# Two up products of an encoder layer: weight sums on another engine, raw weights in other memory, first-half norms in groups, and a sum of squares in two parts

## The chip, the cores and the metric

The kernel runs on one core of one Trainium2 chip. A core has TensorE (PE, matmuls), VectorE (DVE), ScalarE (ACT), GpSimd (POOL) and SyncE (SP, which issues DMAs); each takes its own instructions in program order and waits on semaphores for the others. The metric is the device time of one execution in microseconds (us).

## The reference

One layer of a bidirectional encoder in float32, for 1024 positions and 16 meta tokens in front (1040 rows), width 1024:

```
h += 0.5 * SwiGLU_1(RMSNorm(h))
u  = RMSNorm(h);  z = u @ W_in       # two head groups, differential and windowed attention
h += concat(A, RMSNorm(B)) @ W_out
h += 0.5 * SwiGLU_2(RMSNorm(h))      # then a final RMSNorm
swiglu(x) = (silu(x @ w_gate) * (x @ w_up)) @ w_down      # 1024 -> 2816 -> 1024
rmsnorm(x) = x * rsqrt(mean(x * x) + 1e-6) * g
```

The change is in the two products with `w_gate` and `w_up`, here called the up products.

## The kernel before

**Numbers in halves.** A float32 product is made of three products of high and low parts: `split` makes `hi` by a ScalarE copy and `lo = src - hi` on VectorE (L117 and L114 in the profile; `tt`, L114, is every two-operand sum or difference). An operand is ready for the third pass only with its low part, the remainder.

**The up product.** `ffn_up` is called twice, with 520 rows in a half (two matmuls of 260 columns a step) and with 512. It takes gate and up together as a block product by fewer multiplications: for each of 22 tiles `f` of 128 output columns the weights are four blocks, `a11`, `a12` (the raw tile `rg` of `w_gate`) and `a21`, `a22` (the raw `ru` of `w_up`), and seven products of sums of blocks stand for eight. The sums of weights are `s1 = a21 + a22`, `s2 = s1 - a11`, `a21 = a11 - a21` (written over `ru`, so it appears as `ru<-rg,ru`) and `s4 = a12 - s2` (`s<-rg,s`). Their high and low halves are the tiles `wah`/`wal` (raw `a11`, `a12`, and the first tile's `s2`, `s1`), `wbh`/`wbl` (`s2`, `s1` of later tiles) and `wch`/`wcl` (`a21`, `s4`, `a22`). For the first tile, `f = 0`, `s1` and `s2` are made early by `first_sums` on VectorE; all else is made by GpSimd in the tile loop. The products are in L226, what they leave in PSUM is taken by VectorE into `u` and `g` and by ScalarE into `m` and `sg`.

**The sums of activations.** The other operands are blocks of the normed input: `b11` and `b21` of the first half of the rows, `b22` and `t1` to `t4` of both halves. `prepare` (`prepare1`, `prepare2`) makes the first half, its norm and the splits into `b11` and `b21`; `combine` makes the second half and the rest in `second_half`. The input tiles are called `ha`, `hc` (first half) and `hb`, `hd` (second half), `x2` is a temporary. A norm is a sum of squares over 1024 (squares on ScalarE, the sum over partitions by a matmul with ones), then `newton` (L139 to L142: two steps on ScalarE, the first with a table load, and two on VectorE, written `nr` and `ns`), then one VectorE operation for each tile, `normed` (L149). In the first product `rstd_each` squares eight tiles and lets TensorE add them all, in the second the squares are added on VectorE.

**Order.** `lead_a` and `lead_b` do for the first five tiles the two products that need only `b11` and `b21` and raw blocks, so that TensorE has work while `combine` makes the rest (`early_work` deals them out). A scheduler puts the instructions of each engine in order before the program runs, and small edits change its order. Memory is taken in rings, reserved by name in the order of a table; the rings `la4` of the tile loop lie where the preparation's tiles (`nsq`, `nacc`, `ns`, `nr`, `x2`, `ha` to `hd`) lay, so a load or a split into `la4` waits until the last reader of the tile that was there is done.

Of the kernel before, what the change touches and what calls it, by code (L numbers as in the profile page):

```python
# [10 lines left out]
F32 = mybir.dt.float32  # L11
F32R = mybir.dt.float32r
AF = mybir.ActivationFunctionType
ALU = mybir.AluOpType
# [4 lines left out]
P = 128  # L19
D = 1024  # L20
KT = D // P
# [30 lines left out]
def layer(  # L52
# [4 lines left out]
    nc = tc.nc  # L57
# [55 lines left out]
    def tt(eng, out, a, b, op):  # L113
        eng.tensor_tensor(out, a, b, op=op)  # L114
# [75 lines left out]
    def ffn_up(H, wg, wu, nlead, prepare, combine, accs):  # L190
# [5 lines left out]
        with ExitStack() as st:  # L196
# [103 lines left out]
            for tag, bufs in (  # L300
                ("rg0", 1), ("ru0", 1), ("wbh", 2), ("wbl", 2), ("rg1", 1), ("ru1", 1),
                ("u2", 1), ("m5", 1), ("u3", 1), ("wch", 3), ("wcl", 3), ("g", G_BUFS),
            ):
                la4.reserve(tag, bufs)
# [9 lines left out]
            for f in range(FT):  # L314
# [28 lines left out]
                product(p3, weight(la4, "wb", s1, 2) if f else first["ws1"], "t1", True)  # L343
                tt(gp, a21, a11, a21, ALU.subtract)
                m5 = tmp(la5, "m5")
# [4 lines left out]
                if nxt is not None:  # L350
                    lead_b(nxt, src)
                tt(gp, s4, a12, s2, ALU.subtract)
                product(p3, weight(la5, "wc", s4, 3), "b22", False)
# [37 lines left out]
    def first_half(hts, gi, r, blk):  # L391
        hk = KT // 2
        for k in range(KT):
            hi, lo = blk["b11" if k < hk else "b21"]
            normed(hts[k], hts[k], gi, k, r)
            split(hi[:, k % hk, :], lo[:, k % hk, :], hts[k])
            yield

# [267 lines left out]

    def rstd_each(srcs, n, width, pool, subs, full):

        for i, s in enumerate(srcs):
            sq = pool.tile([P, 520], F32, tag="nsq", name="nsq")[:, :n]  # L670
            nc.scalar.activation(sq, s, AF.Square)
            for o, (c0, cn) in subs:
                nc.tensor.matmul(o, ones, sq[:, c0 : c0 + cn], start=i == 0, stop=i == len(srcs) - 1)
        return newton(n, width, pool, full)

    def prepare1(pool, psum, blk, ps_tile, subs):
# [9 lines left out]
        outs, full = ps_tile("p2")  # L686
        r = rstd_each(a, H, D, pool, list(zip(outs, subs)), full)
        for _ in first_half(a, 0, r, blk):
# [572 lines left out]
    def prepare2(pool, psum, blk, ps_tile, subs):  # L1261
# [3 lines left out]
        with ExitStack() as st_w:  # L1265
            wp = Rings(st_w, "wo2")
            blocks = iter(())
            for half in range(2):
                sl = slice(half * H, (half + 1) * H)
                hs = []  # L1270
                for m in range(KT):
# [15 lines left out]
                    hs.append(t)  # L1287
                    next(blocks, None)
                halves.append(hs)
                if half == 0:  # L1290
# [130 lines left out]
```

## Time and profile before

| what | before |
|---|---|
| time, median of 3 runs | 2092.57 us (2092.17 to 2096.58) |
| the profiled execution's own time | 2091.47 us |
| its span in the profile | 2089.7 us (1.8 us lie around it) |
| mean granted clock of TensorE | 0.973 |
| busy: TensorE / VectorE / ScalarE / GpSimd | 1956.9 / 1262.0 / 882.8 / 993.3 us |

TensorE is busy for 94% of the span. The two up products begin at 24.38 and 1381.44 us of the span. A row of the timeline says when an operation began, how long it took, its engine, line and tiles, and in brackets how long the engine had been idle before it and what ended that. The clock is given as a share of full speed.

### The profile page before, as it was taken

The numbers are of one execution on the slowest core, as the hardware profiler recorded it, in microseconds if no ns is written. First come the engines' busy times: TensorE is split into PE (matmuls) and PEld (weight loads), VectorE is DVE, ScalarE is ACT, GpSimd is POOL, SyncE is SP. The second block draws the span as 40 slices with busy tenths as digits, with TensorE's granted clock in tenths as the row PEclk, the third lists the DMA queues.
The fourth block names the chain that finished last, engine by engine and source line by source line (L and its number), as shares of the span: only waits on it lengthen the run. The fifth ranks groups of instructions, "written<-read, shape, count | busy, mean of one in ns | idle before, by whom it ended". The sixth has DMA issues, their size and how long they took to land. (4 is left out here: it accounts for less than half of the span.)

```text
span 2089.7 us, 30414 instructions
## 1 busy us (share of the span) xinstructions
PE 1956.9 (94%) x11508; PEld 1701.2 (81%) x11508; DVE 1262.0 (60%) x1843; ACT 882.8 (42%) x1611; POOL 993.3 (48%) x811
## 2 busy tenths in 40 slices
PE   6999999998999989899978898897999999989998
PEld 5999999998999879778756677675788888867877
DVE  6755555548874661276668677466655455487745
ACT  6433333334432431366566666353333333344433
POOL 0555554545443740576446442017754554454543
PEclk8999999999999999999979999998999999999999
DMA  4332322328422351544443321522333233385122
GB/s 157 110 118 97 117 91 99 108 94 314 153 62 81 130 165 62 152 118 121 109 102 91 83 75 53 194 92 81 122 106 111 86 106 112 116 297 166 61 81 81
DMA packets 106002, 244.14 MB, mean 117 GB/s; under 512 B 14208, under 2 KB 29008, under 8 KB 105856
## 3 DMA queue, kind: packets, MB, share of 16 engines
q1 hardware_dynamic: 94336, 204.53, 30.9%
q0 software_dynamic: 11520, 37.67, 4.6%
q8 instruction: 90, 1.47, 0.3%
q14 instruction: 56, 0.46, 0.1%
HBM read 169.86 MB, written 65.44 MB: 113 GB/s over the span
## 5 line engine op out<-in xcount | busy, mean ns | idle before, releaser
L226 PE MATMUL p<-t_hi,wch 128*128 128x260 f32 (+1 forms) x528 | 142.9, 325 | 9.4 <-DVE u L114 9.4
L226 PE MATMUL p<-b_hi,wah 128*128 128x260 f32 (+1 forms) x528 | 144.4, 328 | 7.0 <-ACT b_hi L117 3.8
L226 PE MATMUL p<-b_hi,wal 128*128 128x260 f32 (+1 forms) x528 | 142.3, 325 | 6.4 <-DVE wal L114 6.4
L226 PE MATMUL p<-b_lo,wah 128*128 128x260 f32 (+1 forms) x528 | 143.7, 325 | 0.0
L226 PE MATMUL p<-t_lo,wch 128*128 128x260 f32 (+1 forms) x528 | 142.2, 324 | 0.0
L226 PE MATMUL p<-t_hi,wcl 128*128 128x260 f32 (+1 forms) x528 | 141.9, 323 | 0.0
L114 DVE TENSOR_TENSOR u<-p,m 128x520 f32<-128x520 f32 (+1 forms) x88 | 61.0, 693 | 129.2 <-PE p L226 129.1
L114 POOL TENSOR_TENSOR ru<-rg,ru 128x512 f32<-128x512 f32 x44 | 87.6, 1990 | 106.8 <-DVE hb L149 74.0
L226 PE MATMUL p<-t_hi,wbh 128*128 128x260 f32 (+1 forms) x504 | 133.7, 321 | 2.6 <-ACT wbh L117 2.6
L226 PE MATMUL p<-t_lo,wbh 128*128 128x260 f32 (+1 forms) x504 | 135.9, 320 | 0.0
L226 PE MATMUL p<-t_hi,wbl 128*128 128x260 f32 (+1 forms) x504 | 133.3, 320 | 0.0
L117 ACT CAST wch<-ru 128x512 fp32r<-128x512 f32 x88 | 54.8, 623 | 183.8 <-issue 89.5
L574 PE MATMUL pA<-bh,wh 128*128 128x260 f32 (+1 forms) x432 | 116.3, 323 | 5.4 <-DVE h L581 5.4
L117 ACT CAST wbh<-s 128x512 fp32r<-128x512 f32 x84 | 52.3, 622 | 152.1 <-PE p L226 137.3
L574 PE MATMUL pA<-bl,wh 128*128 128x260 f32 (+1 forms) x432 | 115.5, 321 | 0.0
L114 POOL TENSOR_TENSOR s<-ru 128x512 f32<-128x512 f32 x42 | 57.4, 1368 | 120.3 <-DMA ru<-wu 60.9
L574 PE MATMUL pA<-bh,wl 128*128 128x260 f32 (+1 forms) x432 | 112.3, 319 | 0.0
L114 DVE TENSOR_TENSOR bl<-r,bh 128x520 fp32r<-128x520 f32 (+1 forms) x126 | 109.9, 907 | 2.3 <-ACT bh L117 2.0
L114 POOL TENSOR_TENSOR s<-wr 128x384 f32<-128x384 f32 x48 | 55.2, 1153 | 114.0 <-DVE wl L114 94.2
L117 ACT CAST wh<-s 128x384 fp32r<-128x384 f32 x96 | 49.1, 515 | 136.8 <-PE pA L574 66.6
L581 DVE SCALAR_TENSOR_TENSOR h<-pA,h 128x520 f32<-128x520 f32 (+1 forms) x96 | 66.2, 691 | 63.1 <-PE pA L574 63.0
L117 ACT CAST wah<-rg 128x512 fp32r<-128x512 f32 x88 | 54.4, 621 | 117.9 <-PE p L226 89.2
(289 smaller groups left out, 6128.0 us busy)
## 6 DMA issues: line engine op xcount, KB each, us to landing
rg<-wg SPq DMA_DIRECT2D x44, 512.0 KB, 3.6
ru<-wu SPq DMA_DIRECT2D x44, 512.0 KB, 5.2
wr<-wd SPq DMA_DIRECT2D x24, 768.0 KB, 4.4
r<-g_t SPq DMA_DIRECT2D x12, 780.0 KB, 5.9
r<-g_t SPq DMA_DIRECT2D x12, 768.0 KB, 5.8
g_b<-g POOLq DMA_DIRECT2D x27, 260.0 KB, 5.2
r<-g_b SPq DMA_DIRECT2D x9, 780.0 KB, 4.9
g_b<-g POOLq DMA_DIRECT2D x27, 256.0 KB, 5.5
```

The lines of the kernel that those rows point to most:

```text
L114: eng.tensor_tensor(out, a, b, op=op)
L117: nc.scalar.copy(hi, src)
L226: nc.tensor.matmul(o, w_k(ww, k), x[:, k, c0 : c0 + cn], start=first and k == 0 and i == 0, stop=k == hk - 1 and i == 2, skip_group_check= ...
L574: nc.tensor.matmul(o, w_k(ww, k), xx[:, c0 : c0 + cn], start=new and k == 0 and q == 0, stop=k == DNG - 1 and q == 2, skip_group_check=not ...
L581: nc.vector.scalar_tensor_tensor(hs, full, 0.5, hs, op0=ALU.mult, op1=ALU.add)
```

## The change

Four edits, all at the starts of the up products.

1. The rings `rg1` and `ru1` (raw weights of odd tiles) are reserved ahead of `wbh` and `wbl`, so they lie on other tiles of the preparation.
2. For `f = 0` the two sums `a21 = a11 - a21` and `s4 = a12 - s2` are made by VectorE; for later tiles by GpSimd as before.
3. `first_half` norms a group of four tiles and then splits it, for `b11` and then for `b21`, in twice as many steps; `prepare2` takes two steps where it took one.
4. `prepare1` adds its squares by `rstd_pair` (two accumulators, adds on VectorE, then the matmuls with ones), which the second half already used; `rstd_each` is gone.

```diff
             for tag, bufs in (
-                ("rg0", 1), ("ru0", 1), ("wbh", 2), ("wbl", 2), ("rg1", 1), ("ru1", 1),
+                ("rg0", 1), ("ru0", 1), ("rg1", 1), ("ru1", 1), ("wbh", 2), ("wbl", 2),
                 ("u2", 1), ("m5", 1), ("u3", 1), ("wch", 3), ("wcl", 3), ("g", G_BUFS),
...
-                tt(gp, a21, a11, a21, ALU.subtract)
+                tt(gp if f else nc.vector, a21, a11, a21, ALU.subtract)
...
-                tt(gp, s4, a12, s2, ALU.subtract)
+                tt(gp if f else nc.vector, s4, a12, s2, ALU.subtract)
...
     def first_half(hts, gi, r, blk):
         hk = KT // 2
-        for k in range(KT):
-            hi, lo = blk["b11" if k < hk else "b21"]
-            normed(hts[k], hts[k], gi, k, r)
-            split(hi[:, k % hk, :], lo[:, k % hk, :], hts[k])
-            yield
+        for n, ks in (("b11", range(hk)), ("b21", range(hk, KT))):
+            hi, lo = blk[n]
+            for k in ks:
+                normed(hts[k], hts[k], gi, k, r)
+                yield
+            for k in ks:
+                split(hi[:, k % hk, :], lo[:, k % hk, :], hts[k])
+                yield
...
-        r = rstd_each(a, H, D, pool, list(zip(outs, subs)), full)
+        r = rstd_pair(a, H, D, pool, list(zip(outs, subs)), full)
...
                     next(blocks, None)
+                    next(blocks, None)
```

The order of the instructions changes with it. On VectorE at the start of the second product, behind the last two norms (`hb`, `hd`) of the second half, there stood before:

```order
L149 SCALAR_TENSOR_TENSOR hd_15521<-hd_15521,gains_64,nr_15752 128x512
L114 TENSOR_TENSOR ha_15124<-hb_15381,ha_15124 128x512
L114 TENSOR_TENSOR ha_15147<-hb_15401,ha_15147 128x512
L114 TENSOR_TENSOR b22_lo_15576<-hd_15461,b22_hi_15572 128x512
L114 TENSOR_TENSOR ha_15170<-hb_15421,ha_15170 128x512
```

and now:

```order
L149 SCALAR_TENSOR_TENSOR hd_15514<-hd_15514,gains_64,nr_15746 128x512
L114 TENSOR_TENSOR ha_15118<-hb_15375,ha_15118 128x512
L114 TENSOR_TENSOR ru_16063<-rg_16061,ru_16063 128x512
L114 TENSOR_TENSOR ha_15141<-hb_15394,ha_15141 128x512
L114 TENSOR_TENSOR b22_lo_15570<-hd_15455,b22_hi_15566 128x512
```

The sum `ru<-rg,ru` of the first tile, which GpSimd had, is the second row behind the norms; the other moved sum, `s<-rg,s`, is row 34 behind these norms, and the two remainders `wcl` that TensorE needs from them are rows 43 and 44.

On ScalarE, behind the last sigmoid before the second half's norm, there stood before:

```order
L252 ACTIVATE sg_15775<-p1_15705 128x512
L117 CAST wah_15837<-rg0_15835 128x512
L139 ACT_TABLE_LOAD
L139 ACTIVATE nr_15752<-p2_15726,eps_66 128x512
L140 ACTIVATE ns_15751<-nr_15752 128x512
```

and now:

```order
L252 ACTIVATE sg_15769<-p1_15699 128x512
L139 ACT_TABLE_LOAD
L139 ACTIVATE nr_15746<-p2_15720,eps_66 128x512
L117 CAST wah_15831<-rg0_15829 128x512
L140 ACTIVATE ns_15745<-nr_15746 128x512
```

The copy `wah` of a raw weight stood ahead of the table load and the step L139; it now stands between L139 and L140.

On VectorE in the first product, from the third row that makes `t1_lo` on, there stood before, up to the fourth of the weight remainders made from raw blocks in this stretch:

```order
L114 TENSOR_TENSOR t1_lo_322<-ha_208,t1_hi_318 128x520
L114 TENSOR_TENSOR hb_226<-hd_234,hb_226 128x520
L114 TENSOR_TENSOR hc_212<-hc_212,x2_601 128x520
L114 TENSOR_TENSOR t1_lo_322<-ha_210,t1_hi_318 128x520
L114 TENSOR_TENSOR t2_lo_330<-x2_601,t2_hi_326 128x520
L114 TENSOR_TENSOR wal_650<-rg0_647,wah_649 128x512
```

and now:

```order
L114 TENSOR_TENSOR hb_224<-hd_232,hb_224 128x520
L114 TENSOR_TENSOR t1_lo_316<-ha_208,t1_hi_312 128x520
L114 TENSOR_TENSOR hb_226<-hd_234,hb_226 128x520
L114 TENSOR_TENSOR t1_lo_316<-ha_210,t1_hi_312 128x520
L114 TENSOR_TENSOR wal_644<-rg0_641,wah_643 128x512
L114 TENSOR_TENSOR hc_212<-hc_212,x2_595 128x520
L114 TENSOR_TENSOR wal_684<-rg0_681,wah_683 128x512
```

The last row before and the last but two now are the remainder of the same block of weights. From the first norm of the second half (`hb`) to it, that row included, there were 32 rows and are 29: one remainder (`wal_536`, now `wal_530`) went ahead of the norms, and `hc` and `t2_lo` of the first tile went behind it. The first tile's sum `ru<-rg,ru` stands ahead of these norms, among the remainders `b_lo` of the first half.

On SyncE the load of the second tile's `ru` waits for another VectorE row than before: in the second product for the fourth `t2_lo` and no longer for the fourth `x2` and a copy, in the first product likewise for the fourth `t2_lo` instead of the fourth `x2`.

## Rows read from the trace of the kernel before

**Rows 1.** Busy time by stretches: stretch, its us, each engine's busy us, clock, DMA share.
```profile
0.00:50.00 50.00, 30.92 (x158) 26.49 (x159) 33.85 (x55) 30.61 (x51) 4.35 (x10) 0.85 0.46 162
50.00:100.00 50.00, 45.97 (x356) 45.12 (x355) 39.99 (x55) 22.27 (x39) 26.61 (x18) 0.95 0.30 101
100.00:150.00 50.00, 50.00 (x420) 50.00 (x419) 28.44 (x41) 16.79 (x29) 28.63 (x28) 1.00 0.37 128
1345.00:1395.00 50.00, 49.50 (x213) 39.56 (x212) 33.63 (x53) 21.63 (x36) 0.00 (x0) 1.00 0.35 127
1400.00:1450.00 50.00, 33.59 (x111) 23.58 (x111) 39.41 (x61) 23.31 (x40) 36.29 (x9) 0.83 0.20 68
```

**Rows 2.** TensorE's timeline, second product: start, us, line, tiles, [idle before <-releaser].
```profile
1432.13 0.79 PE L226 MATMUL p<-b_hi,wch 128*128 128x512 f32 x1 [5.47 <-ACT wch L117]
...
1436.27 0.80 PE L226 MATMUL p<-t_hi,wch 128*128 128x512 f32 x1 [0.79 <-DVE u L114]
...
1440.13 0.79 PE L226 MATMUL p<-t_hi,wbh 128*128 128x512 f32 x1 [2.64 <-ACT wbh L117]
...
1444.56 0.44 PE L226 MATMUL p<-t_lo,wch 128*128 128x512 f32 x1
...
1455.97 0.50 PE L226 MATMUL p<-t_hi,wbh 128*128 128x512 f32 x1
```

**Rows 3.** GpSimd's timeline, second product.
```profile
1404.94 25.25 POOL L114 TENSOR_TENSOR ru<-rg,ru 128x512 f32<-128x512 f32 x1 [74.00 <-DVE hb L149]
1430.15 1.27 POOL L114 TENSOR_TENSOR s<-rg,s 128x512 f32<-128x512 f32 x1
1438.16 1.26 POOL L114 TENSOR_TENSOR s<-ru 128x512 f32<-128x512 f32 x1 [6.74 <-issue]
```

**Rows 4.** VectorE's timeline, second product.
```profile
1401.40 0.75 DVE L149 SCALAR_TENSOR_TENSOR hb<-hb,gains,nr 128x512 f32<-128x512 f32 x1
...
1406.70 1.29 DVE L114 TENSOR_TENSOR ha<-hb,ha 128x512 f32<-128x512 f32 x2
...
1428.38 0.69 DVE L114 TENSOR_TENSOR hc<-hc,x 128x512 f32<-128x512 f32 x1
1432.63 0.69 DVE L114 TENSOR_TENSOR t_lo<-x,t_hi 128x512 fp32r<-128x512 f32 x1 [3.56 <-ACT t_hi L117]
```

**Rows 5.** ScalarE's timeline, second product.
```profile
1393.62 1.09 ACT L252 ACTIVATE sg<-p 128x512 f32<-128x512 f32 x2
1396.14 0.62 ACT L117 CAST wah<-rg 128x512 fp32r<-128x512 f32 x1 [1.43 <-DMA rg<-wg]
1396.78 1.28 ACT L139 ACT_TABLE_LOAD   x1
...
1430.22 0.62 ACT L117 CAST wch<-ru 128x512 fp32r<-128x512 f32 x1 [4.11 <-POOL ru L114]
```

**Rows 6.** TensorE's timeline, first product.
```profile
47.15 0.51 PE L226 MATMUL p<-b_hi,wal 128*128 128x260 f32 x2 [1.77 <-DVE wal L114]
...
57.51 0.51 PE L226 MATMUL p<-b_hi,wal 128*128 128x260 f32 x2 [2.67 <-DVE wal L114]
...
77.87 0.50 PE L226 MATMUL p<-t_hi,wch 128*128 128x260 f32 x2 [1.32 <-DVE u L114]
```

**Rows 7.** VectorE's timeline, first product.
```profile
36.44 1.71 DVE L149 SCALAR_TENSOR_TENSOR hb<-hb,gains,nr 128x520 f32<-128x520 f32 x1
...
56.78 0.68 DVE L114 TENSOR_TENSOR wal<-rg,wah 128x512 fp32r<-128x512 f32 x1
...
73.11 3.48 DVE L114 TENSOR_TENSOR wcl<-ru,wch 128x512 fp32r<-128x512 f32 x2
```

**Rows 8.** GpSimd's timeline, first product.
```profile
36.30 1.29 POOL L114 TENSOR_TENSOR ru<-rg,ru 128x512 f32<-128x512 f32 x1 [32.17 <-DMA ru<-wu]
```

**Rows 9.** SyncE's queue: issue of loads, both products.
```profile
63.58 0.33 SPq L311 DMA_DIRECT2D ru<-wu  x1
...
1432.35 6.02 SPq L311 DMA_DIRECT2D ru<-wu  x2
```

More of the change, by code (lines that the diff above doesn't have):

```diff
@@ L665, in rstd_pair @@
         return newton(n, width, pool, full)
[L667 to L674, printed above, removed]
     def prepare1(pool, psum, blk, ps_tile, subs):
```

## The prediction

> **What bounds the kernel now.** I read four views in this order. The table by stretches of 50 us first: TensorE is full (50.00 of 50) with the clock at 1.00 in 100 to 150 us, and short of work in two places, the first 100 us and 1400 to 1450 us, where it is busy for 30.92, 45.97 and 33.59 us and the clock falls to 0.85, 0.95 and 0.83 [rows 1]. Both are the starts of an up product: there the inputs are normed and split on VectorE and ScalarE while TensorE already wants them. An edit to these starts pays what TensorE waits less there, so that is read from its waits.
>
> The second view is the timeline of those waits. In the second up product TensorE waits 5.47 us for the high half of a weight sum, 0.79 us for a VectorE sum and 2.64 us for the next tile's high half [rows 2]; in the first, 1.77 and 2.67 us for a weight remainder (`wal`) and 1.32 us for `u` [rows 6].
>
> The third is what stands behind the longest of them. GpSimd's one subtraction `ru<-rg,ru` runs from 1404.94 for 25.25 us, and the like sum after it takes 1.27 us [rows 3]. VectorE, in the same time, runs 36 operations back to back from 1406.70 to 1428.38, 0.602 us apart [rows 4]: it is not slowed, GpSimd is kept out, and the subtraction ends 1.1 us after VectorE's run does. ScalarE's copy then starts at 1430.22, after 4.11 us [rows 5], VectorE's next remainder at 1432.63 [rows 4], TensorE at 1432.13 [rows 2].
>
> The Trainium skill, "SBUF — State Buffer", section "SBUF: two separate sides", says that VectorE and GpSimd share one pair of ports as an exclusive lock, held for a whole instruction, also where a VectorE instruction has two SBUF inputs. The trace agrees in both directions: 25.25 us on GpSimd's side [rows 3], and on VectorE's a first norm of 1.71 us beside a GpSimd sum [rows 7, 8].
>
> The fourth is the order of the two programs (the pieces above), in which I count rows and give each the duration that the trace has for its kind.
>
> **The second up product.** (a) *Its start.* In the new order ScalarE's table load and reciprocal-root step (L139) stand ahead of the copy `wah`, which waited 1.43 us for its load and held them. The table load can start at 1394.71, where the last sigmoid ends, instead of 1396.78; the copy (about 0.5 us) now falls between L139 and L140 [rows 5]. That is 2.07 - 0.5, and I take 1.45 us for VectorE's norms, from 1401.40 to 1399.95; the bound is 0, if TensorE's sum isn't ready or a load is late.
>
> (b) *The two sums on VectorE.* Eight norms take 1406.70 - 1401.40 = 5.30 us [rows 4], so they end at 1405.25. From there to the last remainder that TensorE needs (`wcl` of the second sum) the new order has 44 rows, both moved sums among them, and no GpSimd row that they wait for: 44 x 0.602 = 26.5, so 1431.75. Each sum thus costs VectorE 0.60 us on the path and takes the GpSimd wait away. With that remainder TensorE has done as many matmuls as it had at 1436.27 [rows 2]: a gain of 4.5 us. New, shorter waits will lie ahead of it (about 2 us each, for the high half at 1427.7 and for this remainder); they are inside the 4.5.
>
> (c) *Raw weights of tile 1.* The load of its `ru` was issued at 1432.35 [rows 9] and GpSimd's sum of it started at 1438.16 [rows 3]: 5.8 us. In the new order it waits for the fourth `t2_lo` of VectorE, row 40 of the 44: 1405.25 + 24.1 = 1429.4. With the same 5.8 us it lands at 1435.2; the sum (1.27) and the copy (0.5) give the high half at 1437.0. TensorE wants it 22 matmuls after 1431.75, at 0.233 us each 1436.9, later at half clock. The 2.64 us go.
>
> (d) *The clock.* In the profile, 58 matmuls lie between 1436.27 and tile 2's row at 1455.97. At 0.233 us (the pitch at full clock) they are 13.5 us; they took 19.7. Of the 6.2 lost, 2.64 are the wait, 0.75 two matmuls at half clock before it, 2.1 the ten from 1440.13 to 1444.56 (4.43 us), 0.7 spread after [rows 2]. TensorE still has waits before 1431.75, so I keep the 2.1 and the 0.7 and drop the 0.75. Sum: 4.5 + 2.64 + 0.75 = **7.9 us**. Bounds: no half clock at all, 10.7; no gain at the start, twice the half-clock loss and 0.5 us left of the wait, 7.9 - 1.45 - 2.1 - 0.5 = 3.9.
>
> **The first up product.** *The sum by two accumulators* puts adds on VectorE and takes 24 of 32 ones-matmuls off TensorE. It starts no sooner: the inputs land too late, and ScalarE's L139 step now stands behind a square of the second half. I get the first norm 0.7 us later; but of three VectorE rows between norms and remainders (0.6 each) one is left, so the remainders start 0.5 us earlier. TensorE's gain from that ends in its next wait for `wal`, hence 0 by itself.
>
> *VectorE's run.* Ahead of the second half's norms now stand the `ru` sum and one `wal` (+1.2), less the 0.5: they start at 37.1 instead of 36.44 (+0.7). The GpSimd sum at 36.30, beside which the first norm took 1.71 us [rows 7, 8] and not 0.75 as others do [rows 4], is gone (-1.0). To the `wal` for which TensorE waited 2.67 us there are 29 rows instead of 32, by the order: -3 x 0.6 = -1.8. It starts 2.1 us earlier, at 54.7 [rows 7], and TensorE goes on at 55.4 instead of 57.51 [rows 6].
>
> *The wait for `u`* (1.32 us): `u` was behind two remainders of 3.48 us, slowed beside GpSimd's sums [rows 7]. In the new order it is 28 rows behind that `wal`, ahead of all that need GpSimd's tile-1 sums: 54.7 + 28 x 0.6 = 71.5, ready at 72.2. TensorE asked 19.0 us after that `wal` (77.87 - 1.32 - 57.51 [rows 6]), half-clock loss included, so now at 74.4. The wait goes. The load of tile 1's `ru` becomes later here, behind VectorE's fourth `t2_lo` (66.9 instead of 63.58 [rows 9]): this load isn't helped by the new order of memory. Its sum would be ready near 73, and TensorE needs it near 83. Sum: 2.1 + 1.3 = **3.4 us**; bounds 0 (the `wal`s that follow become late in their turn) and 5.5 (2.1 of half clock gone too).
>
> **Norms before splits, twice as many steps in the second preparation:** TensorE is busy 49.50 of 50 us there [rows 1], so I take 0, within 0.3 either way; the work that hides it is the output projection's matmuls.
>
> **Sum.** 7.9 + 3.4 = 11.3 us off the profiled execution's 2091.47 is 2080.2; that execution lay 1.1 below the median of 2092.57, so **2081.3**. Behind both places TensorE is full, so I see nothing that gives it back. What a measurement here can tell from no change is 0.2%, 4.2 us.
>
> **Rivals.**
> 1. *VectorE becomes the bound.* It takes two sums more, is continuous from 1399.95 to 1433, and what it makes late is the next remainder. For: TensorE's wait on VectorE's `u` [rows 2] and on `wal` [rows 6], and the lower bounds of both places. Against: GpSimd's 25 us cost more than two rows. Time: 2092.57 - 3.9 = 2088.7.
> 2. *The stall moves to GpSimd's next sum,* tile 1's `s<-ru`, kept out by VectorE's run. For: 25.25 us [rows 3], and a run two rows longer. Against: its load lands when the run ends. If it costs 2 us at each place: 2085.3. By the rule of the lock it would end at most one sum after the run.
> 3. *The other side: TensorE's clock stays at half* behind the new waits. At half a matmul of 512 columns takes 0.44 us against 0.233 [rows 2]. The 11.3 us are gone when 54 more of them run at half than now. If all 58 of the second place do (48 more, 10 us) and 140 of the first (0.1 us each at half the columns, 14, of which 2 are lost now): 2092.57 - 11.3 + 22 = 2103. Against: the longest such stretch is 4.4 us in rows 2, behind longer waits.
> 4. *It does not last:* TensorE comes to a later point earlier and waits there for a load or a sum that is tied to something else. Time about 2091. Against: it is full from 100 us on [rows 1].
>
> **How the numbers follow.** Forecast 0.70, rival 1 0.13, rival 2 0.06, rival 3 0.04, rival 4 0.07. Faster by over 0.2% (below 2088.4): forecast, rival 2 and half of rival 1, 0.83; within 0.2%: the rest of rival 1 and rival 4, 0.13; slower: 0.04. The range takes the upper bounds of both places together, 10.7 + 5.5, to 2076.4, and rival 1 at the other end, 2088.7.
>
> **What would show it.** Right: no GpSimd subtraction over 5 us in the second start; the norms there 1.45 us earlier (beside the 3.4 of the first place); TensorE's 5.47 us replaced by two waits of about 2; the 2.64 gone; tile 2 some 8 us earlier against the product's start. In the first product that `wal` near 55 and no wait for `u`. Wrong: waits on `wal` or `t_lo` that grow by as much, a GpSimd sum of over 5 us elsewhere, or a half-clock stretch over 5 us behind the new waits.

## The result and the profile after

The changed kernel takes 2072.26 us (median of 4 runs, 2068.98 to 2074.79) against 2092.37 of the kernel before in the same comparison (4 runs, 2090.39 to 2096.58): a ratio of 0.9904, 95% interval 0.9886 to 0.9922. It is faster, by 20.1 us where 11.3 were forecast, and lies 4.1 us below the forecast range. The two profiled executions took 2091.47 and 2074.79 us, 16.7 apart. The other 3.4 us are where they stand in their runs: the one of before is 0.9 under its median, the one of after 2.5 over its own.

Where the 16.7 lie is read by matching matmuls, counted back from the end of each product, in the two timelines. TensorE is 3.4 us earlier after the start of the first product, 5.8 at the first matmul of the down product behind it, 7.2 when the second product's preparation takes its last sum, 16.3 behind the start of that product (from 1521 us of the profile before on), and 16.7 at the end.

The stretches of 50 us of the changed kernel, to be read beside [rows 1] (columns: stretch, its us, busy time of TensorE, its weight loads, VectorE, ScalarE, GpSimd, clock, DMA share):

```profile
0.00:50.00 50.00, 26.72 (x140) 22.33 (x140) 38.22 (x64) 30.59 (x52) 3.05 (x9) 1.00 0.52 178
50.00:100.00 50.00, 46.41 (x378) 45.47 (x378) 40.53 (x56) 22.48 (x40) 25.50 (x19) 1.00 0.28 96
1390.00:1440.00 50.00, 40.16 (x148) 29.12 (x147) 43.64 (x67) 26.36 (x44) 14.30 (x10) 0.90 0.23 74
```

From 50 to 100 us TensorE does 378 matmuls where it did 356, and the clock is 1.00 in both early stretches. In the second product's start (the window is taken 10 us earlier, as the norms come 9.9 us earlier) it does 148 where it did 111, and GpSimd's busy time falls from 36.29 to 14.30 us with one instruction more.

TensorE's timeline in that start, the answer to [rows 2]:

```profile
1399.23 0.50 PE L226 MATMUL p<-b_hi,wah 128*128 128x512 f32 x1 [1.47 <-ACT sg L252]
...
1419.25 0.50 PE L226 MATMUL p<-b_hi,wch 128*128 128x512 f32 x1 [1.90 <-ACT wch L117]
...
1423.54 0.80 PE L226 MATMUL p<-b_hi,wcl 128*128 128x512 f32 x1 [1.31 <-DVE wcl L114]
...
1427.12 0.40 PE L226 MATMUL p<-b_lo,wch 128*128 128x512 f32 x1
```

The 5.47 us for `wch` have become 1.90 and, for the remainder behind it, 1.31; the 2.64 us for `wbh` are gone; the half clock behind the waits ends at 1427.12, 3.6 us after the second. GpSimd, VectorE and ScalarE in the same place ([rows 3], [rows 4], [rows 5]):

```profile
1425.62 1.30 POOL L114 TENSOR_TENSOR s<-ru 128x512 f32<-128x512 f32 x1 [101.04 <-DMA ru<-wu]
```

```profile
1391.48 0.75 DVE L149 SCALAR_TENSOR_TENSOR hb<-hb,gains,nr 128x512 f32<-128x512 f32 x1
...
1397.39 0.68 DVE L114 TENSOR_TENSOR ru<-rg,ru 128x512 f32<-128x512 f32 x1
...
1416.66 0.68 DVE L114 TENSOR_TENSOR s<-rg,s 128x512 f32<-128x512 f32 x1
...
1422.80 0.68 DVE L114 TENSOR_TENSOR wcl<-s,wch 128x512 fp32r<-128x512 f32 x1
```

```profile
1386.42 1.28 ACT L139 ACT_TABLE_LOAD   x1
...
1388.30 0.61 ACT L117 CAST wah<-rg 128x512 fp32r<-128x512 f32 x1
```

GpSimd has no sum until 1425.62, and that one takes 1.30 us. Each moved sum takes VectorE 0.68 us. From the first norm to the end of the remainder VectorE takes 32.0 us; the forecast had 31.8 (1399.95 to 1431.75). The first norm is 9.9 us earlier than in [rows 4]: 7.2 by the earlier arrival and 2.7 here. The copy `wah` stands behind L139's step, as the order said.

The first product, on TensorE and on VectorE ([rows 6], [rows 7]):

```profile
45.70 0.51 PE L226 MATMUL p<-b_hi,wal 128*128 128x260 f32 x2 [1.98 <-DVE wal L114]
...
55.46 0.51 PE L226 MATMUL p<-b_hi,wal 128*128 128x260 f32 x2 [1.94 <-DVE wal L114]
```

```profile
37.16 0.75 DVE L149 SCALAR_TENSOR_TENSOR hb<-hb,gains,nr 128x520 f32<-128x520 f32 x1
...
54.73 0.68 DVE L114 TENSOR_TENSOR wal<-rg,wah 128x512 fp32r<-128x512 f32 x1
...
72.36 0.70 DVE L114 TENSOR_TENSOR u<-p,m 128x520 f32<-128x520 f32 x1 [0.55 <-PE p L226]
```

The norms start at 37.16 (forecast 37.1), the `wal` at 54.73 (54.7), TensorE goes on at 55.46 (55.4), and `u` is ready before TensorE asks.

The end of the first product was in no group of rows. TensorE's wait there, before and after:

```profile
487.34 0.51 PE L226 MATMUL p<-t_hi,wch 128*128 128x260 f32 x2 [3.73 <-DVE u L114]
```

```profile
482.62 0.50 PE L226 MATMUL p<-t_hi,wch 128*128 128x260 f32 x2 [2.41 <-DVE u L114]
```

The last product of a tile, `t4`, adds onto the accumulator that VectorE must first have read into `u`. That read stands, in VectorE's order, behind splits of the down product.

### The profile page after: what moved, and what is told of

It reads as the page before. It is cut to its first block, busy times and chain, and to the rows that moved or that the text cites. A ratio compares the mean times of both kernels' runs of the same rounds, so it can differ in the third digit from the quotient of the medians.

```text
span 2072.9 us, 30356 instructions
## 1 busy us (share of the span) xinstructions
PE 1943.9 (94%) x11484; PEld 1692.1 (82%) x11484; DVE 1279.3 (62%) x1853; ACT 879.4 (42%) x1611; POOL 960.3 (46%) x807
## 3 DMA queue, kind: packets, MB, share of 16 engines
q8 instruction: 90, 1.47, 0.3%
## 4 chain that ended last, share of the span: by engine, by line
PE 70%; DVE 11%; DMA 6%; ACT 5%; POOL 3%; issue 3%; SPq 1%; DVEq 0%; POOLq 0%; ACTq 0%
PE p L226 35%; PE pA L577 7%; PE pj L167 5%; PE pC L577 3%; PE pv L884 3%; PE pd L167 2%; PE ds L780 2%; DVE bl L114 2%; PE po L167 2%; PE do L1183 2%; PE pB L577 2%; PE do L167 1%; DMA ru<-wu 1%; POOL s L114 1%; ACT dp L786 1%
## 5 line engine op out<-in xcount | busy, mean ns | idle before, releaser
L114 DVE TENSOR_TENSOR wal<-rg,wah 128x512 fp32r<-128x512 f32 x88 | 74.0, 847 | 63.6 <-ACT wah L117 63.6
L117 ACT CAST wch<-ru 128x512 fp32r<-128x512 f32 x88 | 54.7, 621 | 130.5 <-PE p L226 72.6
L114 POOL TENSOR_TENSOR s<-wr 128x384 f32<-128x384 f32 x48 | 55.4, 1157 | 100.6 <-DVE wl L114 89.7
```

The lines of the kernel that those rows point to most:

```text
L117: nc.scalar.copy(hi, src)
```

## The experiments

In the tables each time is a median, beside that of the kernel before on the same chip. Places are differences of matched matmuls against the profile of before, in us (minus is earlier). "First start" is read behind the start of the first product, where the difference no longer changes (150 to 450 us of the profile before), "first end" at the first matmul of the down product; "second start" is counted from the second preparation's last sum to the stretch from 1521 to 1639 us of the profile before, where the differences hold still again.

| run | time | before | ratio (95%) | first start | first end | second start |
|---|---|---|---|---|---|---|
| e1 before again | 2092.05 | 2090.82 | 1.0012 (1.0002 to 1.0021) | -0.1 | +0.2 | -0.3 |
| e2 sums alone | 2083.46 | 2090.82 | 0.9968 (0.9957 to 0.9980) | +0.2 | +0.3 | -6.0 |
| e3 all but sums | 2078.66 | 2090.82 | 0.9939 (0.9918 to 0.9961) | -2.2 | -4.6 | -6.4 |
| e4 one sum alone | 2091.26 | 2090.82 | 1.0001 (0.9989 to 1.0013) | -0.5 | -0.2 | -0.7 |
| e5 rings alone | 2081.58 | 2091.69 | 0.9943 (0.9924 to 0.9962) | -1.7 | -2.5 | -4.0 |
| e6 norms alone | 2087.77 | 2091.69 | 0.9982 (0.9969 to 0.9996) | -0.4 | +0.7 | -2.4 |
| e7 pair alone | 2088.42 | 2091.69 | 0.9986 (0.9974 to 0.9999) | -1.7 | -0.5 | -0.5 |
| e8 all but norms | 2076.96 | 2091.69 | 0.9924 (0.9906 to 0.9941) | -3.5 | -5.8 | -5.2 |
| e9 all but rings | 2081.29 | 2091.62 | 0.9948 (0.9934 to 0.9962) | -1.4 | -1.3 | -9.6 |
| e10 all but pair | 2078.23 | 2091.62 | 0.9938 (0.9921 to 0.9955) | +1.3 | +0.2 | -8.1 |
| e11 low parts on GpSimd | 2076.18 | 2091.62 | 0.9930 (0.9915 to 0.9945) | -1.7 | -2.7 | -7.0 |
| e12 changed again | 2071.95 | 2091.62 | 0.9912 (0.9897 to 0.9927) | -2.2 | -4.6 | -9.0 |
| e13 rings, second product only | 2085.19 | 2090.26 | 0.9977 (0.9966 to 0.9987) | -0.5 | +0.7 | -3.7 |
| e14 before, own accumulator | 2091.82 | 2090.26 | 1.0006 (0.9993 to 1.0019) | -0.2 | -1.5 | -1.3 |
| e15 changed, own accumulator | 2075.41 | 2090.26 | 0.9929 (0.9915 to 0.9942) | -2.7 | -3.8 | -8.9 |

The first profile of the changed kernel, the one of the section on the result, has -3.4, -5.8 and -9.1 in the last three columns.

**e1 and e12: what two profiles of one kernel differ by.** No edit.

> The kernel of before, unchanged, profiled once more. Of the profiled gain of 16.7 us, 2.5 lie at the end of the first up product, where TensorE waits 3.73 us for VectorE's last sum in before and 2.41 us in the changed kernel, and about 1 us in the down product behind it. Theory (these belong to the change): the wait at the end is again 3.7 us within 0.3, and the median within 0.2% of before. Rival (such waits vary from run to run): the wait at the end differs by over 1 us from 3.73, and stages between 490 and 1390 us shift by 1 us or more against the first profile.

> The changed kernel once more, for the spread of its profile. Theory: its stages are within 1 us of the first profile up to 500 us and inside the second product; what differs lies in the attention stage between 730 and 1320 us, by 1 to 3 us as in the two profiles of before. Rival: the stages at the products' starts differ by over 1 us too, and then the single terms can't be read to better than that.

In e1 the wait at the first product's end is again 3.73 us, as its theory says. In e12 the first start differs by 1.2 us from the first profile, so there the rival holds, and the clock of the first 100 us is another one:

```profile
0.00:50.00 50.00, 27.09 (x137) 22.60 (x137) 37.60 (x63) 30.05 (x51) 3.06 (x9) 0.83 0.53 178
50.00:100.00 50.00, 47.03 (x371) 46.20 (x372) 39.72 (x56) 22.74 (x40) 25.22 (x18) 0.97 0.30 95
```

So the 1.00 and 1.00 of the first profile are not the change's. The places move by up to 1.3 us between two profiles of the same kernel, the stretches behind them (attention, the second down product) by up to 3, and single runs of one kernel by up to 14 (e9: 2073.82 to 2088.22). So a place is read to about 1 us, and what an edit is worth in all is read from medians. These have an error too: the unchanged kernel of e1 lies 1.2 us off itself, with an interval that does not take in 1. The gain came again: 2071.95.

**e2, e3, e4: the sums.**

```diff
-                tt(gp, a21, a11, a21, ALU.subtract)
+                tt(gp if f else nc.vector, a21, a11, a21, ALU.subtract)
-                tt(gp, s4, a12, s2, ALU.subtract)
+                tt(gp if f else nc.vector, s4, a12, s2, ALU.subtract)
```

e2 is the kernel before with both pairs of lines, e4 with the first pair alone, e3 the changed kernel without both.

> Only the first tile's two weight sums go to VectorE; rings, norms and the sum of squares stay as before. Theory (GpSimd is kept out by VectorE's run, and that is most of the gain in the second product): no GpSimd sum over 5 us there, TensorE's waits of 5.47 and 2.64 us shrink to under 5 together, the second product's start gains 5 to 8 us, the whole 6 to 12 us: 2080 to 2086. Rival (VectorE is the bound; the gain came from the other three edits): under 3 us in all, 2089 or more, with waits on VectorE's remainders grown by what was saved.

> The changed kernel with both sums of the first tile back on GpSimd. Theory: GpSimd's sum in the second product again takes over 20 us, until VectorE's run ends, and the second product loses 7 to 10 us against the changed kernel; what stays is the first product's start and the earlier norms, 2 to 8 us under before: 2084 to 2090. Rival (the sums matter little): within 3 us of the changed kernel, 2070 to 2076.

> Only the sum written over ru goes to VectorE; the other, s4, stays on GpSimd, all else as before. Theory (VectorE's back-to-back run keeps GpSimd out as long as it lasts): s4 starts inside the run and takes until about its end, 5 to 12 us and not 1.3, and TensorE waits longer for its high half than with both sums moved: 1 to 4 us slower than that kernel. Rival (the lock is given to GpSimd after at most one VectorE operation): s4 takes under 3 us and the time is that of both sums moved, within 1 us.

GpSimd and TensorE in the second start of e3:

```profile
1395.37 24.68 POOL L114 TENSOR_TENSOR ru<-rg,ru 128x512 f32<-128x512 f32 x1 [70.49 <-DVE hd L149]
```

```profile
1422.00 0.79 PE L226 MATMUL p<-b_hi,wch 128*128 128x512 f32 x1 [5.47 <-ACT wch L117]
```

TensorE's wait is back to the hundredth, with all else changed. The second start loses 2.7 us by it (-6.4 where the changed kernel has -9.1) and the whole 6.7 against e12: less than the 7 to 10 of the theory, more than the 3 of the rival. In e4, where only `ru` is VectorE's, GpSimd and TensorE:

```profile
1425.43 7.67 POOL L114 TENSOR_TENSOR s<-rg,s 128x512 f32<-128x512 f32 x1 [91.71 <-DVE wal L114]
```

```profile
1433.79 0.80 PE L226 MATMUL p<-b_hi,wch 128*128 128x512 f32 x1 [4.11 <-ACT wch L117]
...
1441.63 0.79 PE L226 MATMUL p<-t_hi,wbh 128*128 128x512 f32 x1 [3.05 <-ACT wbh L117]
```

The other sum now falls into VectorE's run and takes 7.67 us, as the theory said and not under 3. It costs more than the 1 to 4 us expected: e4 is 7.8 slower than e2, and the whole gain is gone. In e2, with both moved, TensorE:

```profile
1429.90 0.50 PE L226 MATMUL p<-b_hi,wch 128*128 128x512 f32 x1 [0.54 <-ACT wch L117]
...
1436.86 0.50 PE L226 MATMUL p<-t_hi,wbh 128*128 128x512 f32 x1 [0.43 <-ACT wbh L117]
```

So the sums alone take the long wait, and with the old order of memory also all but 0.43 of the 2.64 us. Place and time (6.0 and 7.4 us) are as the theory says.

**e5, e9, e13: the rings.** e5 is the kernel before with the new order of memory, e9 the changed kernel with the old one, e13 the kernel before with the new one in the second product only.

```diff
-                ("rg0", 1), ("ru0", 1), ("wbh", 2), ("wbl", 2), ("rg1", 1), ("ru1", 1),
+                ("rg0", 1), ("ru0", 1), ("rg1", 1), ("ru1", 1), ("wbh", 2), ("wbl", 2),
```

```diff
-                ("rg0", 1), ("ru0", 1), ("wbh", 2), ("wbl", 2), ("rg1", 1), ("ru1", 1),
+                ("rg0", 1), ("ru0", 1),
+                *((("wbh", 2), ("wbl", 2), ("rg1", 1), ("ru1", 1)) if two else (("rg1", 1), ("ru1", 1), ("wbh", 2), ("wbl", 2))),
```

> Only the order of the rings changes: rg1 and ru1 ahead of wbh and wbl. The kernel with all but the sums had lost TensorE's 2.64 us wait for tile 1's high half though GpSimd was kept out for 24.68 us. Theory (the rings free tile 1's raw weights earlier): that wait of 2.64 us shrinks below 1 us, the 5.47 us stays within 0.5, the second start gains 2 to 3 us, the whole 2 to 4: 2087 to 2089. Rival (the loads follow GpSimd's late sum whatever memory they take): the wait stays at 2 us or more and the time within 1.5 us of before.

> The changed kernel with the rings in their old order. Rings alone had given 10 us: TensorE's 1.32 us for u and 2.64 us for tile 1's high half went, the norms of the second product came earlier, and the last sum of the first product was waited for by 2.58 us and not 3.73, with the down product behind it some 2 us sooner. Theory (the ends of the product belong to the rings, the starts are shared with the other edits): the wait at the end of the first product is again 3.7 us, the wait for tile 1's high half stays under 1 us since the sums are gone from GpSimd, the whole loses 4 to 8 us against the changed kernel: 2076 to 2080. Rival (the rings' gain is all at the starts, where the other edits give it too): within 2 us of the changed kernel and 2.4 us of wait at the end.

> The kernel before with the new order of memory in the second up product alone; the first product keeps the old order. Theory (the order of memory pays in both products: alone it gave 10.1 us, of which the second start is some 4): the wait of 2.64 us goes and tile 2 of the second product stands some 4 us earlier, the wait for u of 1.3 us near 77 and the wait of 3.73 us at the end of the first product stay; time some 5 us under the kernel before, 2086.5. Rival (all of it is paid in the second product and what stands behind it): time some 9 to 10 under, 2082, as with both.

e5 gains 10.1 us where 2 to 4 were expected. e13 gains 5.1, as expected: half of the 10.1 goes with the order in the second product, half with that in the first. e9 loses 9.3 us against e12, more than the 4 to 8 of its theory; its waits are as that theory says. VectorE at the end of the first product, before and then in e5:

```profile
478.57 2.99 DVE L114 TENSOR_TENSOR bl<-r,bh 128x520 fp32r<-128x520 f32 x2
481.48 1.37 DVE L114 TENSOR_TENSOR wl<-s,wh 128x384 fp32r<-128x384 f32 x1
482.77 0.69 DVE L114 TENSOR_TENSOR u<-p,u 128x520 f32<-128x520 f32 x1
483.38 3.29 DVE L114 TENSOR_TENSOR wl<-s,wh 128x384 fp32r<-128x384 f32 x3
486.60 0.69 DVE L114 TENSOR_TENSOR u<-p,m 128x520 f32<-128x520 f32 x1
```

```profile
477.78 0.90 DVE L114 TENSOR_TENSOR bl<-r,bh 128x520 fp32r<-128x520 f32 x1
...
483.73 0.69 DVE L114 TENSOR_TENSOR u<-p,m 128x520 f32<-128x520 f32 x1
```

The scheduler has put one `bl` of the down product further ahead, from between the two reads to before the first of them, and VectorE's run reaches the last `u` 2.9 us earlier; only 1.7 of these came with the start. TensorE there in e5, e9 and e13:

```profile
484.47 0.50 PE L226 MATMUL p<-t_hi,wch 128*128 128x260 f32 x2 [2.58 <-DVE u L114]
```

```profile
76.50 0.51 PE L226 MATMUL p<-t_hi,wch 128*128 128x260 f32 x2 [1.30 <-DVE u L114]
...
485.95 0.80 PE L226 MATMUL p<-t_hi,wch 128*128 128x260 f32 x2 [3.73 <-DVE u L114]
```

```profile
77.34 0.51 PE L226 MATMUL p<-t_hi,wch 128*128 128x260 f32 x2 [1.11 <-DVE u L114]
...
486.83 0.80 PE L226 MATMUL p<-t_hi,wch 128*128 128x260 f32 x2 [3.74 <-DVE u L114]
```

With the old order in the first product both waits for `u` are there in these two, at 76 to 78 us and at the end; with the new one, in e5, the first is gone and the second shorter. For the wait at the end that holds in all kernels in the table whose last tile is as before: 3.73 or 3.74 us in e1, e2, e4, e6, e7, e9 and e13, and 2.41 to 2.58 in the changed kernel, e3, e5, e8, e10, e11 and e12. For the first wait it does not: with the old order it is missing in e2, e4 and e7, which wait 0.53 us for `wah` some 8 us earlier, and with the new one it is there in e11 (1.10 us).

From the first start to the first end the changed kernel, e3, e8 and e12 all gain 2.4 us, e5, e10 and e11 0.7 to 1.1; the kernels with the old order there and the last tile as before gain nothing, and some lose up to 1.2. The shorter wait is 1.2 to 1.3 us of this, and TensorE's clock is the rest: the 24 matmuls behind the wait take 2.99 or 3.00 us, all at full clock, in the four that gain 2.4, and 4.3 to 4.5, about half of them at half clock, in e5, e10 and e11 (4.10 in the kernel before). Why the clock holds in four of them was not tested.

In e5's profile the lead then grows from 2.5 us to 4.1 behind the down product and to 7.1 at the second preparation's last sum. That is not read as the rings': between 767 and 1324 us, in attention, the places move by +2.7 (e4) to -4.0 us (e15) in kernels without an edit there. The second product's start is as early in e9 (-9.6) as in the changed kernel (-9.1): beside the moved sums the rings bring nothing there.

**e14, e15: is that wait itself worth money?** In the last tile `t4` goes into an accumulator of its own, and VectorE adds the two (one row more in each product); e14 is the kernel before with it, e15 the changed kernel.

```diff
-                product(p2, weight(la5, "wc", a22, 3), "t4", False)
+                last = f == FT - 1
+                p4, p4f = ps_tile("p1") if last else (p2, p2f)
+                product(p4, weight(la5, "wc", a22, 3), "t4", last)
                 g1 = tmp(la5, "g", G_BUFS)
                 tt(nc.vector, g1, p2f, m1, ALU.add)
+                if last:
+                    tt(nc.vector, g1, p4f, g1, ALU.add)
```

> The kernel before; for the last tile of each up product the t4 product goes into an accumulator of its own (p1, which no later tile needs) and VectorE adds the two, so that TensorE doesn't wait there until VectorE has read p2 into u. One VectorE row more in each product. Theory (the 3.73 us wait at 487.34 and the half clock behind it, some 1.3 us, are TensorE's wait for VectorE's read of p2, behind bl and wl rows of the next stage; and this place was open to gain): the wait is gone, the down product's first matmul is some 4 to 5 us earlier, and with the second product's 2.44 the time is 3 to 7 us under the kernel before, 2086 to 2089. Rival (the down product's first operands are made by the same VectorE rows and are late anyway): the wait moves to bl or wl, the time stays within 2 us of the kernel before.

> The changed kernel with the same edit (t4 of the last tile in an accumulator of its own). Theory: the waits for u of 2.41 us at 482.62 and 1.99 us at 1822.78 go with the half clock behind them: 2 to 5 us under the changed kernel, 2067 to 2070. Rival (the wait moves to bl or wl): 2072, as the changed kernel, within 2 us.

e14 is no faster than the kernel before, as the rival says. e15 gains 14.9 us, some 5 less than the changed kernel: neither its theory nor its rival had it that slow. TensorE, VectorE and GpSimd at that place in e14:

```profile
489.94 0.77 PE L578 MATMUL pA<-bh,wh 128*128 128x260 f32 x2 [3.63 <-DVE u L114]
```

```profile
481.28 5.24 DVE L114 TENSOR_TENSOR wl<-s,wh 128x384 fp32r<-128x384 f32 x4
...
489.11 0.68 DVE L114 TENSOR_TENSOR u<-p,u 128x520 f32<-128x520 f32 x1
```

```profile
482.31 1.21 POOL L114 TENSOR_TENSOR s<-wr,s 128x384 f32<-128x384 f32 x1
```

TensorE does the `t4` matmuls at once and then waits 3.63 us at the first matmul of the down product, again for VectorE's `u` and not for the `bl` or `wl` of the rival. Which accumulator it waits for makes no difference: VectorE is late there, its four `wl` taking 1.31 us each. What could pay at this place is less work for VectorE ahead of that row; no run tried it.

**e6, e8: norms before splits.** e6 is the kernel before with the edit, e8 the changed kernel without it.

```diff
-        for k in range(KT):
-            hi, lo = blk["b11" if k < hk else "b21"]
-            normed(hts[k], hts[k], gi, k, r)
-            split(hi[:, k % hk, :], lo[:, k % hk, :], hts[k])
-            yield
+        for n, ks in (("b11", range(hk)), ("b21", range(hk, KT))):
+            hi, lo = blk[n]
+            for k in ks:
+                normed(hts[k], hts[k], gi, k, r)
+                yield
+            for k in ks:
+                split(hi[:, k % hk, :], lo[:, k % hk, :], hts[k])
+                yield
...
                     next(blocks, None)
+                    next(blocks, None)
```

> Only the first half's norms and splits go in groups, with two steps where one was taken in the second preparation. I had put 0 on this edit. In the changed kernel the second half's norms of the second product came 3.0 us earlier against the product's entry, twice what I had taken. Theory: this edit alone makes them 1.5 to 3 us earlier and TensorE's stalls ahead of 1411 us shorter; 1 to 3 us in all: 2088 to 2090. Rival (it was hidden, as predicted): norms within 0.5 us of before against the entry, time within 1 us of before.

> The changed kernel with the first half's norms and splits one by one again, one step in the second preparation. Theory (the norms' groups make the second start's norms earlier): the second product loses 1.5 to 3 us against the changed kernel and the first little: 2073 to 2076. Rival (hidden): within 1 us of the changed kernel, 2071 to 2073.

The edit, costed at 0, gives 3.9 us alone, and without it the changed kernel gains 14.7 instead of 20.1 (19.7 in e12). In e6 the second start moves 2.4 us. ScalarE and VectorE there, behind the preparation's last sum at 1391.82:

```profile
1393.09 1.28 ACT L139 ACT_TABLE_LOAD   x1
...
1394.97 0.61 ACT L117 CAST wah<-rg 128x512 fp32r<-128x512 f32 x1
```

```profile
1398.15 0.75 DVE L149 SCALAR_TENSOR_TENSOR hb<-hb,gains,nr 128x512 f32<-128x512 f32 x1
```

So it is this edit that puts the copy `wah` behind L139's step, and the norms come 6.33 us behind the sum instead of 8.60, as the theory of e6 says. That holds in every kernel of the table: 5.87 to 6.36 us with the edit, 7.82 to 9.10 without it, e8 (7.96) among the latter. In e8 TensorE is thus 1.8 us later than in the changed kernel at the matmul that stood at 1436.86 in the profile before, but only 0.5 at that of 1446.01, and then it loses its lead at one row:

```profile
1442.21 0.50 PE L226 MATMUL p<-t_hi,wch 128*128 128x512 f32 x1 [3.15 <-DVE u L114]
```

**e7, e10: the sum of squares in two parts.** e7 is the kernel before with it, e10 the changed kernel without it.

```diff
-        r = rstd_each(a, H, D, pool, list(zip(outs, subs)), full)
+        r = rstd_pair(a, H, D, pool, list(zip(outs, subs)), full)
```

> Only the first product's sum of squares goes by two accumulators. Theory: by itself it is worth 0 to 1.5 us at 79 us (its gain ends in the next wait for a weight remainder), and the end of the first product, where VectorE's last sum waited behind three remainders of the down product, is as before: 2089 to 2091. Rival: it gives the whole 2 us that the kernel with all but the sums had gained by 79 us, and the 2.2 us at that product's end: 2086 to 2088.

> The changed kernel with the first product's sum of squares by 32 matmuls again. Alone the edit had taken 3.3 us off, of it 1.4 to 2 us by 79 us. Theory (the shorter run of VectorE rows in front of the waits for weight remainders comes with it): the first start loses 1 to 2 us, nothing changes from 100 us on: 2073 to 2075. Rival (hidden, as predicted, and the run's rows come from the other edits): the first start within 0.5 us of the changed kernel.

It moves the first start by 1.7 us alone, and without it the changed kernel is 6.3 slower (2078.23 against e12's 2071.95) and loses its whole lead there (level with the kernel before up to 100 us, and 1.3 behind it after a wait of 1.02 us for `wah` at 105.00). That is more than both forecasts of e10 allow. Alone, 1.2 of its 1.7 us are gone at the first end: TensorE waits the same 3.73 us for `u`, until 485.62, and the 24 matmuls behind it run at half clock up to 490.92, 5.30 us where the kernel before took 4.10 (487.34 to 491.44).

**e11: two low parts of `t4` on GpSimd.** An attempt at a faster version: the changed kernel, with two VectorE rows less in front of `wcl`.

```diff
-        def parts(n, j, src):
+        def parts(n, j, src, eng=None):
-            split(hi, lo, src)
+            split(hi, lo, src, eng)
-            parts("t4", j, firsts[j + hk])
+            parts("t4", j, firsts[j + hk], nc.gpsimd if j >= 2 else None)
```

> The changed kernel with the last two low parts of t4 made on GpSimd, which waits idle for VectorE's run to end. It computes the same. VectorE's run gets two rows (1.2 us) shorter ahead of the remainder that TensorE waits 1.31 us for. Theory (VectorE's run is what bounds the start now): that remainder is 0.6 to 1.2 us earlier in both products, 1 to 2 us in all, tile 1's sum on GpSimd begins later but under 1 us is lost by it: 2070 to 2072. Rival (GpSimd's two rows are kept out until the run ends and delay tile 1's sum, wanted at once): TensorE waits over 1 us for tile 1's high half and the time is that of the changed kernel or 1 to 3 us more.

It is 4.2 us slower than the changed kernel (e12). GpSimd, VectorE and TensorE:

```profile
1416.48 3.43 POOL L114 TENSOR_TENSOR t_lo<-hc,t_hi 128x512 fp32r<-128x512 f32 x2 [94.77 <-ACT t_hi L117]
```

```profile
1419.36 1.69 DVE L114 TENSOR_TENSOR wcl<-ru,wch 128x512 fp32r<-128x512 f32 x2 [1.82 <-ACT wch L117]
```

```profile
1421.71 0.80 PE L226 MATMUL p<-b_hi,wcl 128*128 128x512 f32 x1 [2.88 <-DVE wcl L114]
```

VectorE has fewer rows and now stands idle for 1.82 us: ScalarE's `wch` (1418.71) waits 1.11 us for GpSimd's `t_lo`, presumably because it goes into memory that `hc` had. TensorE's wait grows from 1.31 to 2.88. The theory fails; the rival comes nearer, but the wait that it named, for tile 1's high half, is not there, and the loss is larger.

No version tried beats the changed kernel.

## Why the forecast was too small

The direction, the place of the largest gain and its mechanism were right, and the two starts together, 12.5 us in the profile, lie within their bounds of 16.2. What took the time out of the range lies outside the two starts and, for 3.4 us, in where the profiled executions stand in their runs.

**The second start: forecast 7.9, measured 9.1.** Term (b), the starved GpSimd sum, is shown by e2, e3 and e4: it has the 1.45 of (a) inside, so by itself it is 3.05, and in e3 the second start loses 2.7 with the sums back on GpSimd. VectorE's chain from the norms to the remainder was sized to 0.2 us, and "two waits of about 2" were 1.90 and 1.31. Term (a) was mis-sized, by too little: against the preparation's last sum (1392.80 before, 1385.61 after) the norms came at 8.60 ([rows 4], 1401.40) and now at 5.87, 2.7 us earlier instead of 1.45. The copy `wah` did fall between L139 and L140, as costed; but the sigmoids ahead of L139, which had ended 1.91 us behind that sum, now end 0.80 behind it (1386.41), because the copies ahead of them wait 1.46 us for their load instead of 3.04, here before and after:

```profile
1391.16 1.14 ACT L117 CAST wah<-rg 128x512 fp32r<-128x512 f32 x2 [3.04 <-DMA rg<-wg]
```

```profile
1382.56 1.14 ACT L117 CAST wah<-rg 128x512 fp32r<-128x512 f32 x2 [1.46 <-DMA rg<-wg]
```

With 2.7 for the 1.45 the terms give 9.15, what was measured. The edit that makes (a) is the norms in groups (e6, e8), the one of which the prediction says "I take 0, within 0.3 either way": it saw the new order of the rows, but not which edit it came from. Term (c) named one of two edits that each do it: the 2.64 us go with the sums alone (e2, 0.43 left) as well as with the rings alone, so in the change the rings bring nothing more at that place (e9).

**The first start: forecast 3.4, measured 3.4** in the one profile and 2.2 in the other. "It starts no sooner ... hence 0 by itself", said of the sum of squares, was wrong: alone it gives 1.7 there (e7), without it nothing is left (e10). That 3.4 was met exactly is luck in part: the sum kept all of the half clock, and the first profile has a clock of 1.00 in both early stretches. In e12, with 0.83 and 0.97, the norms start at 37.80, TensorE goes on at 56.10 behind that `wal`, and 2.2 are left. The wait for `u` is gone in both, but also in kernels with other edits (e2, e4, e5 and e7).

**The step that failed** is the reading that TensorE is "short of work in two places, the first 100 us and 1400 to 1450 us", with "Behind both places TensorE is full, so I see nothing that gives it back" in the sum: what lies outside the two starts had no term, neither gained nor lost. The stretches of 50 us that I read were those around the starts, and the trace had a wait of 3.73 us for `u`, with half clock behind it, at 487.34. There VectorE, not TensorE, sets the time (e14, e15), and with the new order of memory VectorE's run reaches it earlier (e5 against e9 and e13). That gave 2.4 us at the first product's end in the profile, 1.3 of them the shorter wait and 1.1 the full clock behind it. By the medians about half of the rings' 10.1 us goes with the order in that product (e5 less e13: 5.0 us), and only part of this was found in rows.

**The sum.** The median's gain exceeds the forecast by 8.8 us: 1.2 in the second start, 2.4 at the first product's end, 1.8 in the stretches between and behind, 3.4 from where the two profiled executions stand in their runs. The last is no property of the kernel: one execution was taken as a fixed 1.1 us from the median, and these kernels scatter by several.

**The rivals.** 1, VectorE as the bound, is true of the waits that remain in both starts and of the first product's end, but each is shorter than what was removed. 2, the stall moving to GpSimd's next sum, did not come: tile 1's `s<-ru` took 1.30 us. In e4 it moves to the other sum of the first tile, which the change had moved as well. 3, half clock, lasted 3.6 us behind the new waits, against a loss of 2.1 and 0.7 that was kept. 4, a gain that doesn't last, is what the sum of squares alone does at the first product's end (e7).

**What stays open.** The edits alone give 7.4, 10.1, 3.9 and 3.3 us, 24.7 in all where together they give 20.1; part of the overlap is named above, but what the sum of squares and the norms give beyond the two starts (up to 3 us in the medians) was found at no row. Why the down product behind the first up product takes one to three microseconds less in several kernels is also open: the order of VectorE's splits there changes with each edit, and what that does was followed at one place only (the `bl` at the first product's end).

## What to carry to other kernels

Here an operation of GpSimd that fell into a long back-to-back run of two-operand VectorE work took the rest of that run, so move all that fall there or none: moving one of two gained nothing. When a new order of rows is read for its price, find out which edit makes it. When an edit shortens a start, look at every wait of TensorE up to the next start for an engine that sets the time there, and list the waits by size over the whole span before calling a stretch full. Edits whose waits overlap aren't worth their sum, and one profiled execution isn't its kernel's median.

## What the runs showed of the hardware

One subtraction that takes 1.3 us by itself was kept out for 25.25, 24.68 and, as the other sum, 7.67 us (before, e3, e4), each time until 1.1 us behind the end of VectorE's run, and VectorE lost nothing by it. It did not wait for a result of that run: in the changed kernel the same two subtractions run on VectorE in the middle of it (1397.39 and 1416.66). The prediction took the 25.25 us as agreeing with the rule of the lock, but they are more than it gives. The Trainium skill, "SBUF — State Buffer", section "SBUF: two separate sides", has the lock held for one instruction at a time; by that alone, as an estimate, the sum would wait for one VectorE operation, 0.6 us, and not for all of the 36 that the prediction counts. The measurement decides: in these three runs GpSimd did not get in between two VectorE operations that follow each other without a gap.

That is no rule for every such run. In e14 VectorE's four `wl` follow each other without a gap too, at 1.31 us each, and beside them GpSimd's sums take 1.21 to 1.47: there VectorE is the one that waits. The same kind of row with GpSimd idle, in the profile before:

```profile
498.32 0.55 DVE L114 TENSOR_TENSOR wl<-wr,wh 128x384 fp32r<-128x384 f32 x1
```

What decides which of the two engines waits was not tested.
